# A hybrid RWKV and attention layer: GpSimd's tiles behind the key norm, final states ahead of the third pair's operands, and the MLP norm by a ones matrix

## Chip, core and metric

The kernel runs on one core of one Trainium2 chip. The metric is the device time of one execution in microseconds. TensorE is called PE, VectorE DVE, ScalarE ACT, GpSimd POOL and SyncE SP.

## What is computed

One layer for 512 prompt tokens and 8 sequences of 8 decode tokens. RWKV-7 mixing and differential attention run side by side on the same normalised input; gates merge them; a squared-ReLU MLP and a final norm follow. Of the reference, what the change touches:

```python
kk = hs((k * lp['k_k']).astype(f32))
kk = kk / jnp.maximum(jnp.linalg.norm(kk, axis=-1, keepdims=True), 1e-12)
...
def step(S, inp):                     # one token of the RWKV scan
    sa = jnp.einsum('bhij,bhj->bhi', S, a_t)
    S = S * w_t[:, :, None, :] + sa[..., None] * b_t[:, :, None, :] + v_t[..., None] * k_t[:, :, None, :]
    return S, jnp.einsum('bhij,bhj->bhi', S, r_t)
...
x = x + m @ lp['w_out']
hn = rmsnorm(x, lp['g_ffn'], NORM_EPS)
x = x + jnp.square(jax.nn.relu(hn @ lp['w_up'])) @ lp['w_down']
return x, S, ...                      # S: the final states, an output
```

The norm's factor commutes with the squared ReLU: with m the mean square plus epsilon, the MLP's sum is 1/m times that of the unscaled row. So the kernel multiplies x by m (M2), adds the products of the unscaled row, and multiplies by 1/m (R2) at the end.

## The kernel before

Tokens lie on the free axis: 576 columns, in two spans of 288 (HALF). Weights come in pieces through a ring of three loads, and each is split into a high and a low part (ACT makes `hi`, L179, DVE `lo`, L180), so that every product is three matmuls. Small helpers record the instructions, and the trace shows their lines: `act` L58, `tt` L61, `stt` L66, `ts` L69, `mm` L72, `tr` (transpose on PE) L76. `bank` hands out one of three PSUM banks.

The RWKV part works on four pairs of heads, hp 0 to 3 (first to fourth pair). `rwkv(hp)` is a generator in six stages, cut by `yield`:

1. The key norm: squares `sq`, their sums by PE into `pn`, `nr` by DVE, the power -1/2 by GpSimd (L760), the copy `nb` over 64 columns a head by GpSimd (L763), and PE transposes of it into `pk` and `pks`. PE makes the adapters' products `pw` and `pa` meanwhile. DVE scales the keys (`sq` again), builds `rkp`, whose block sums are `pbn`, and the operands KB and ST. GpSimd zeroes half of ST (L818). PE multiplies them into `pA`.
2. The values SVU; KBt; the start states `s0` of the decode rows, loaded over SP (L859) into one of two buffers; their products `pI`. GpSimd fills two parts of SVU (L871, L872).
3. The inverse of the triangular blocks, TT; GpSimd zeroes parts of it (L923, L924).
4. The final states of the decode rows: GpSimd makes `vm` (L933), PE `pF`, DVE adds and scales in the buffer of `s0`, and a DMA from GpSimd's queue writes it out (L941).
5. and 6. The mean and variance of the output rows, and the output.

`chain(pr)` (L991) runs the recurrence over eight prompt chunks and the decode chunk for two pairs at once; the chunk steps are short dependent products with DVE and ACT copies between them (`pch`, `R`, `SVU`, `S`). The code below the generators (L1081 on) calls stages and chains, with `take(n)` to put n matmuls of waiting dense products (`ps_z`, `ps_g`) between. Each product has a priority, and a scheduler orders every engine's instructions by priority and by the order in which they are written; `tc.issue_after` ties instructions to one given.

Ahead of the MLP, `acc` holds the squares of x summed over the eight blocks of 128 channels. `up_pair` makes seven products of twelve matmuls each (`ua`, `ub`, `uc`, `ud`, `ux`; a 2x2 product scheme), `down` the products `ps_dn`. After the first `up_pair`, `colsum` sums `acc` over the partitions with ten narrow matmuls into `pst`, DVE makes m (128x5) and its reciprocal r, and `spread` turns each back into rows of 576 by five PE transposes (`pb_M`, `pb_R`) and five ACT copies.

Of the kernel before, what the change touches and what calls it, by code (L numbers as in the profile page):

```python
# [8 lines left out]
F32 = mybir.dt.float32  # L9
# [6 lines left out]
P = 128  # L16
D = 1024
# [11 lines left out]
HALF = ((0, 288), (288, 288))  # L29
# [7 lines left out]
C_ID, C_OB, C_M, C_MS, C_LM, C_I32, C_HS, C_SEL, C_MB, C_CM, C_END = (  # L37
    0, 128, 256, 384, 512, 672, 704, 706, 738, 746, 748)
# [3 lines left out]
def tile_hybrid_step(ctx, tc, xT, xsT, ktab, vtab, s0T, ptab, w_in, vecs, w2a2, g2, lamv,  # L42
# [3 lines left out]
    PE, VE, AE, GE = nc.tensor, nc.vector, nc.scalar, nc.gpsimd  # L46
    PS = bass.MemoryType.PSUM

    def pool(name, bufs=1, stack=ctx, **kw):
        return stack.enter_context(tc.tile_pool(name=name, bufs=bufs, **kw))  # L50
# [4 lines left out]
    ring = {"job": 0}  # L55

    def act(out, in_, func=AF.Copy, **kw):
        ring["act"] = AE.activation(out=out, in_=in_, func=func, **kw)  # L58

    def tt(out, a, b, op, eng=None):  # L60
        ins = (eng or VE).tensor_tensor(out=out, in0=a, in1=b, op=op)  # L61
        if eng is None:
            ring["tt"] = ins

    def stt(out, a, s, b, op0, op1):
        VE.scalar_tensor_tensor(out=out, in0=a, scalar=s, in1=b, op0=op0, op1=op1)  # L66

    def ts(out, a, s1, op0, s2=None, op1=ALU.bypass, eng=None):
        (eng or VE).tensor_scalar(out=out, in0=a, scalar1=s1, scalar2=s2, op0=op0, op1=op1)  # L69

    def mm(out, lhsT, rhs, start=True, stop=True):
        ring["mm"] = PE.matmul(out=out, lhsT=lhsT, rhs=rhs, start=start, stop=stop)  # L72
        return ring["mm"]

    def tr(out, in_, idn):
        ring["mm"] = PE.transpose(out=out, in_=in_, identity=idn)  # L76

    def bc(ap, shape):
        return ap.broadcast_to(shape)
# [3 lines left out]
    FEED, LATE, FILL = -1000000, 500000, 1000000  # L83

    @contextmanager
    def prio(at):
        was, tc.cur_priority = tc.cur_priority, at
        yield
        tc.cur_priority = was

    MUL, ADD, SUB, MAX = ALU.mult, ALU.add, ALU.subtract, ALU.max
# [7 lines left out]
    stat = pool("stat", 2)  # L99

    def bank(name):
        return psw.tile([P, 512], F32, tag="w", name=name)

    def tbank(name):
        return psc.tile([P, 512], F32, tag="t", name=name)
# [6 lines left out]
    c = const.tile([P, C_END], F32, name="cst_sb")  # L112
# [3 lines left out]
    ones1 = const.tile([P, 1], F32, name="ones1")  # L116
# [8 lines left out]
    onesP = const.tile([P, P], F32, name="onesP")  # L125
# [90 lines left out]
    def take(n):  # L216

        while waiting and n:
            if next(waiting[0], None) is None:
                waiting.pop(0)  # L220
            else:
                n -= 1
# [11 lines left out]
    def colsum(out, src, sel, n):  # L234

        for t in range(5):
            m = min(P, NT - t * P)
            mm(out[:m, t * n:(t + 1) * n], src[:, t * P:t * P + m], sel)
# [6 lines left out]
    def spread(dst, r, name):  # L245

        for t in range(5):
            m = min(P, NT - t * P)
            pb = bank(f"pb_{name}_{t}")
            tr(pb[:, :m], bc(r[:m, t:t + 1], [m, P]), ident[:m, :m])  # L250
            act(dst[:, t * P:t * P + m], pb[:, :m])
# [19 lines left out]
    with tc.tile_pool(name="xin", bufs=2, reuse_waits="tile") as xin:  # L271
        xt = [xin.tile([P, NT], F32, name=f"x{k}", bufs=1) for k in range(KT)]
        xs_ = xin.tile([P, KT, NB], F32, name="xs", bufs=1)
        acc = xin.tile([P, NT], F32, name="acc", bufs=1)
# [3 lines left out]
        for k in range(0, KT, 4):  # L278
            for j in range(3):
                with prio(FEED + 1000 + 10 * k + j):  # L280
                    name = f"raw_{'qkv'[j]}0_{k}"
# [26 lines left out]
        pst = tbank("pst1")  # L308
# [356 lines left out]
    for h in range(HB):  # L665
        if h:
            qkv(h)
        for cc in range(2):
            GE.tensor_copy(
                out=qbd[64 * cc:64 * cc + 64, :, h, 8 * cc:8 * cc + 8],  # L670
                in_=qT[64 * cc:64 * cc + 64, h, NPR:].rearrange("p (b q) -> p b q", b=NB))
# [47 lines left out]
    def ch(a):  # L719
        return a.rearrange("p (c t) -> p c t", t=64)  # L720
# [21 lines left out]
    def rwkv(hp):  # L742
        e = hp % 2
        own = pair.setdefault(hp // 2, {})
        hs = slice(hp * P, (hp + 1) * P)
        r, k, vv = Pt[hp], Pt[4 + hp], Pt[8 + hp]
# [8 lines left out]
        for t, o in enumerate(toks):  # L755
# [4 lines left out]
        GE.tensor_tensor(out=nr, in0=nr, in1=mhalf[:, :10], op=ALU.pow)  # L760

        nb = rt.tile([P, 5, P], F32, tag="G", name=f"nb{hp}", bufs=3)
        GE.tensor_copy(out=nb.rearrange("p t (a d) -> p (t a) d", a=2),  # L763
                       in_=nr.rearrange("p (a o) -> p a o", o=1).broadcast_to([P, 10, 64]))
        u = tmp("u")
        aa = tmp("aa")
# [47 lines left out]
        for par, rows in halves:  # L814
            stt(KB[rows, :, par], ch(aa)[rows], 0.5, ch(pinv)[rows], MUL, MUL)
            tt(KB[rows, :, 1 - par], ch(k2)[rows], ch(pinv)[rows], MUL)
            st = rb_.tile([P, NCH, 2, 64], F32, tag=f"ST{par}", name=f"ST{par}_{hp}")
            GE.memset(st[64 - 64 * par:128 - 64 * par], 0.0)  # L818
            stt(st[rows, :, 0], ch(kk)[rows], -1.0, ch(pm)[rows], MUL, MUL)
            tt(st[rows, :, 1], ch(r)[rows], ch(pe)[rows], MUL)  # L820
            ST.append(st)
# [4 lines left out]
        for par in range(2):  # L826
            rows = slice(64 * par, 64 * par + 64)
# [14 lines left out]
        SVU = own["SVU"][:, :, e]  # L842
# [23 lines left out]
        for par in range(2):  # L866
            rows = slice(64 * par, 64 * par + 64)
            for a in range(2):
                act(ST[par][rows, 8, a].rearrange("p (b t) -> p b t", b=NB),
                    pI[rows, 0:P].rearrange("p (b a t) -> p b a t", b=NB, a=2)[:, :, a])  # L870
            GE.tensor_copy(out=SVU[rows, 8, par], in_=c[rows, C_ID + 64 * par:C_ID + 64 * par + 64])  # L871
            GE.memset(SVU[rows, 0, par], 0.0)  # L872

        yield

# [21 lines left out]
        for l in range(1, 5):  # L897

            n = NCH if l < 3 else 8
# [6 lines left out]
        TT = rb_.tile([P, NCH, 64], F32, tag="TT", name=f"TT{hp}")  # L906
# [12 lines left out]
        for b0, b1 in quads:  # L919
            act(TT[b0, :8, 32:64], pC[b0, :256].rearrange("p (c s) -> p c s", c=8))  # L920
            act(TT[b0, :, 0:32], Y[b0])
            act(TT[b1, :, 32:64], Y[b1])
            GE.memset(TT[b0, 8:, 32:64], 0.0)  # L923
            GE.memset(TT[b1, :, 0:32], 0.0)  # L924

        own[e] = ST, KBt, TT, ABR, pc
        yield
# [140 lines left out]


    gens = [rwkv(hp) for hp in range(4)]  # L1070

    def run(*stages):
        for hp in stages:
            while Pt[8 + hp] is None:
                take(2)
            next(gens[hp], None)
# [7 lines left out]
    take(106)  # L1084
    run(1)
    chain(0)
    run(2, 0, 1)
    take(190)
    run(2, 3)
    take(85)  # L1090
# [49 lines left out]
    R2 = fp.tile([P, NT], F32, name="R2")  # L1140
    M2 = fp.tile([P, NT], F32, name="M2")
    acc = fp.tile([P, NT], F32, name="acc2")
# [146 lines left out]
    def down(c, ds):  # L1289

        q, half = divmod(c, 2)
        his, los = ([qs[4 * c + k][:, i] for k in range(4)] for i in range(2))
        for d in ds:
            if c == 0:
                with prio(FEED + 1000 * ring["job"] + 150):
                    tt(ya[:, d], ya[:, d], M2, MUL)

            def ev(ps, t0, n, d=d):
                o = ya[:, d, t0:t0 + n]
                tt(o, o, ps, ADD)  # L1300
            dense(w_down[q, d][:, 4 * half:4 * half + 4], 4, his, los, HALF, ev, f"dn{c}{d}")

    for ch in range(8):
        for i in range(2):
            up_pair(4 * ch + 2 * i)
            if ch == 0 and i == 0:
                with prio(FILL + 1000 * ring["job"] + 999):

                    pst = bank("pst2")
                    colsum(pst, acc, ones1, 1)  # L1310
                with prio(FEED + 1000 * ring["job"]):
                    m2 = stat.tile([P, 5], F32, tag="r", name="m2")
                    r2 = stat.tile([P, 5], F32, tag="s", name="r2")
                    VE.memset(m2, 1.0)
                    ts(m2[:, 0:4], pst[:, 0:4], 1.0 / D, MUL, 1e-6, ADD)
                    ts(m2[:64, 4:5], pst[:64, 4:5], 1.0 / D, MUL, 1e-6, ADD)
                    VE.reciprocal(out=r2, in_=m2)
                with prio(FILL + 1000 * ring["job"] + 1999):
                    spread(M2, m2, "M2")
                with prio(FILL + 1000 * ring["job"] + 9999):  # L1320
                    spread(R2, r2, "R2")
            if 0 < ch < 7:
                down(ch - 1, range(4 * i, 4 * i + 4))

# [2 lines left out]
    rows = []  # L1327
    for d, n in enumerate((None, "t1", "b11", "t2", "b21", "t3", "b22", "t4")):
        if n:
            t = fp.tile([P, 2, 4, 288], F32R, tag=f"h_{n}", name=f"w3_{d}", bufs=1)  # L1330
            t = t.rearrange("p i k t -> p (i k t)")
# [6 lines left out]
    for t0, n in LAST:  # L1338
# [41 lines left out]
        for i, src in enumerate([acc[:, span]] + last):  # L1380
            pst = bank(f"pst3{t0}{i}")
# [20 lines left out]
        for d in range(KT):  # L1402
# [4 lines left out]
            if d + 1 in ends:  # L1407
                i = ends.index(d + 1)
# [119 lines left out]
```

## Time and profile before

| | us |
|---|---|
| median of three runs | 998.73 (998.32 to 999.4) |
| profiled execution | 1002.8 |
| its span, first to last instruction | 1001.0 |
| PE busy | 968.1 |
| DVE busy | 691.0 |
| ACT busy | 496.0 |
| GpSimd busy | 88.6 |

The mean granted TensorE clock is 0.988 of full speed. In a row of the timeline stand the start, the duration, the engine, the line, the operation, output and input by the program's names, the tile's shape and the count; a bracket holds the idle time of the engine ahead of it and what ended that. In the chain of waits stand start, duration and what the time went to. The windows give busy time by engine in a stretch.

### The profile page before, as it was taken

To read this page: it belongs to the slowest core of one execution; us is meant where nothing else is said; L and a number is where in the kernel's file an instruction comes from. 1 tells how busy PE (TensorE), PEld (TensorE's weight loads), DVE (VectorE), ACT (ScalarE), POOL (GpSimd) and SP (SyncE) were. 2 spreads that over 40 slices of the span, in tenths; PEclk is the share of its full clock that TensorE was granted. 3 is DMA by queue.
4 is the path that set the end of the run, shared out by engine and by line. 5 is a ranking of instruction groups with operands and counts; after the bars stand their busy time and mean duration, and the time that the engine had idled before them with its cause. 6 is when DMAs were issued, how large, how long until landed. Compare 5 with 4: busy or idle time off the path is not lost.

```text
span 1001.0 us, 24421 instructions
## 1 busy us (share of the span) xinstructions
PE 968.1 (97%) x10012; PEld 916.7 (92%) x10012; DVE 691.0 (69%) x1459; ACT 496.0 (50%) x1094; POOL 88.6 (9%) x171
## 2 busy tenths in 40 slices
PE   8999999899999989999999999999999999999996
PEld 8999998898887878888889999999999999999996
DVE  6698566774946759536589798966666666666744
ACT  6576455354445344444334666644444444444732
POOL 2511001401002231001110000000000000000001
PEclk9999999999999989999999999999999999999998
DMA  7322673211121225222377642222222222221402
GB/s 264 135 74 76 211 219 112 70 56 54 44 66 38 69 87 160 76 64 102 120 225 237 216 132 86 84 95 86 85 94 86 85 85 85 85 84 44 135 3 95
DMA packets 50833, 105.75 MB, mean 106 GB/s; under 512 B 6066, under 2 KB 8114, under 8 KB 50594
## 3 DMA queue, kind: packets, MB, share of 16 engines
q1 hardware_dynamic: 47442, 96.95, 30.2%
q0 software_dynamic: 1648, 5.35, 1.5%
q10 hardware_dynamic: 1632, 1.89, 0.5%
q8 instruction: 79, 1.29, 0.5%
q14 instruction: 32, 0.26, 0.1%
HBM read 89.38 MB, written 14.78 MB: 104 GB/s over the span
## 4 chain that ended last, share of the span: by engine, by line
PE 88%; DVE 4%; ACT 4%; issue 1%; DMA 1%; POOL 1%; SPq 0%; DVEq 0%; ACTq 0%; POOLq 0%
PE ps_dn L72 21%; PE ps_g L72 10%; PE ps_z L72 8%; PE ua L1247 5%; PE ux L1247 5%; PE ps_wo L72 4%; PE pch L1007 3%; PE ps_brb L72 3%; PE ps_k L72 3%; PE uc L1247 3%; PE ud L1247 3%; PE ub L1247 3%; PE ps_bra L72 3%; PE ps_q L72 2%; PE ps_v L72 2%; PE pA L72 2%
## 5 line engine op out<-in xcount | busy, mean ns | idle before, releaser
L72 PE MATMUL ps_dn<-q,hi_dn 128*128 128x288 f32 x768 | 154.7, 296 | 0.0
L72 PEld LDWEIGHTS ps_dn<-q,hi_dn 128*128 128x128 f32 x768 | 122.7, 188 | 1.4
L72 PE MATMUL ps_dn<-q,lo_dn 128*128 128x288 f32 x384 | 113.1, 295 | 0.0
L72 PE MATMUL ps_g<-xl,hi_g 128*128 128x288 f32 x256 | 79.8, 312 | 0.0
L72 PE MATMUL ps_g<-xh,hi_g 128*128 128x288 f32 x256 | 79.5, 311 | 0.0
L72 PE MATMUL ps_g<-xh,lo_g 128*128 128x288 f32 x256 | 78.3, 306 | 0.0
L72 PEld LDWEIGHTS ps_dn<-q,lo_dn 128*128 128x128 f32 x384 | 72.0, 188 | 0.0
L72 PE MATMUL ps_z<-xh,lo_z 128*128 128x288 f32 (+1 forms) x224 | 69.2, 310 | 0.0
L72 PE MATMUL ps_z<-xh,hi_z 128*128 128x288 f32 (+1 forms) x224 | 68.0, 304 | 0.0
L72 PE MATMUL ps_z<-xl,hi_z 128*128 128x288 f32 (+1 forms) x224 | 67.1, 300 | 0.0
L61 DVE TENSOR_TENSOR ya<-ya,ps_dn 128x288 f32<-128x288 f32 x96 | 43.3, 451 | 29.4 <-PE ps_dn L72 29.4
L58 ACT ACTIVATE hi_dn<-raw_dn 128x512 fp32r<-128x512 f32 x48 | 30.1, 627 | 57.0 <-PE ps_dn L72 57.0
L1247 PE MATMUL ua<-h_b,hi 128*128 128x288 f32 x256 | 53.2, 298 | 0.0
L1247 PE MATMUL ux<-h_t,hi 128*128 128x288 f32 x256 | 52.3, 296 | 0.0
L58 ACT ACTIVATE c<-c 128x288 f32<-128x288 f32 x112 | 48.3, 439 | 7.5 <-DVE c L61 5.9
L72 PEld LDWEIGHTS ps_g<-xh,hi_g 128*128 128x128 f32 x256 | 48.8, 191 | 3.1 <-issue 1.6
L72 PEld LDWEIGHTS ps_g<-xl,hi_g 128*128 128x128 f32 x256 | 49.1, 192 | 1.5
L72 PEld LDWEIGHTS ps_g<-xh,lo_g 128*128 128x128 f32 x256 | 49.0, 191 | 1.0
L58 ACT ACTIVATE hi<-a 128x1024 fp32r<-128x1024 f32 (+1 forms) x32 | 27.1, 845 | 42.0 <-PE ps_dn L72 34.3
L72 PE MATMUL ps_dn<-q,w 128*128 128x320 f32 (+1 forms) x336 | 46.3, 297 | 0.0
L61 DVE TENSOR_TENSOR lo<-s,hi 128x1024 fp32r<-128x1024 f32 x32 | 39.2, 1224 | 10.2 <-ACT hi L58 10.0
L72 PEld LDWEIGHTS ps_dn<-q,w 128*128 128x128 f32 x336 | 45.3, 190 | 0.1
(393 smaller groups left out, 2788.8 us busy)
## 6 DMA issues: line engine op xcount, KB each, us to landing
a<-in_w_up_dram SPq DMA_DIRECT2D x32, 512.0 KB, 3.3
raw_dn<-in_w_down_dram SPq DMA_DIRECT2D x64, 256.0 KB, 2.8
raw_g<-in_w_in_dram SPq DMA_DIRECT2D x32, 256.0 KB, 3.0
raw_z<-in_w_in_dram SPq DMA_DIRECT2D x28, 256.0 KB, 3.0
gt_d<-gg SPq DMA_DIRECT2D x16, 288.0 KB, 2.3
g<-gt_d SPq DMA_DIRECT2D x16, 288.0 KB, 3.6
kp<-in_ktab_dram SPq DMA_DIRECT2D x16, 256.0 KB, 3.7
vp<-in_vtab_dram SPq DMA_DIRECT2D x16, 256.0 KB, 3.9
```

Source lines behind the costliest of these rows:

```text
L58: ring["act"] = AE.activation(out=out, in_=in_, func=func, **kw)
L61: ins = (eng or VE).tensor_tensor(out=out, in0=a, in1=b, op=op)
L72: ring["mm"] = PE.matmul(out=out, lhsT=lhsT, rhs=rhs, start=start, stop=stop)
L1007: ring["mm"] = PE.matmul(out=ps[rows, e], lhsT=lhs, rhs=rhs, start=first and e == 1, stop=True, skip_group_check=True)
L1247: ring["mm"] = PE.matmul(out=ps[:, :288], lhsT=l[:, k], rhs=hb[blk][:, h, k], start=start and i == 0, stop=i == 11, skip_group_check=skip)
```

## The change

Three edits. GpSimd's fills of ST (first pair), and of SVU and TT (first two pairs), are tied behind the copy `nb` of the same pair. Stage 4 of the first two pairs is written ahead of stage 1 of the third. And the MLP norm's column sums are made by a 128x128 matrix of ones, which leaves the sum on every partition at once: M2 comes from it by one operation of DVE on each span, and R2 by a full-width reciprocal, two chunks of the MLP later.

```diff
-        GE.tensor_copy(out=nb.rearrange("p t (a d) -> p (t a) d", a=2),
+        own["nb"] = GE.tensor_copy(out=nb.rearrange("p t (a d) -> p (t a) d", a=2),
...
-            GE.memset(st[64 - 64 * par:128 - 64 * par], 0.0)
+            with tc.issue_after(own["nb"].ins) if hp == 0 else nullcontext():
+                GE.memset(st[64 - 64 * par:128 - 64 * par], 0.0)
...
-            GE.tensor_copy(out=SVU[rows, 8, par], in_=c[rows, C_ID + 64 * par:C_ID + 64 * par + 64])
-            GE.memset(SVU[rows, 0, par], 0.0)
+            with tc.issue_after(own["nb"].ins) if hp < 2 else nullcontext():
+                GE.tensor_copy(out=SVU[rows, 8, par], in_=c[rows, C_ID + 64 * par:C_ID + 64 * par + 64])
+                GE.memset(SVU[rows, 0, par], 0.0)
...
-            GE.memset(TT[b0, 8:, 32:64], 0.0)
-            GE.memset(TT[b1, :, 0:32], 0.0)
+            with tc.issue_after(own["nb"].ins) if hp < 2 else nullcontext():
+                GE.memset(TT[b0, 8:, 32:64], 0.0)
+                GE.memset(TT[b1, :, 0:32], 0.0)
...
     chain(0)
-    run(2, 0, 1)
+    run(0, 1, 2)
...
             if ch == 0 and i == 0:
-                with prio(FILL + 1000 * ring["job"] + 999):
-
-                    pst = bank("pst2")
-                    colsum(pst, acc, ones1, 1)
-                with prio(FEED + 1000 * ring["job"]):
-                    m2 = stat.tile([P, 5], F32, tag="r", name="m2")
-                    r2 = stat.tile([P, 5], F32, tag="s", name="r2")
-                    VE.memset(m2, 1.0)
-                    ts(m2[:, 0:4], pst[:, 0:4], 1.0 / D, MUL, 1e-6, ADD)
-                    ts(m2[:64, 4:5], pst[:64, 4:5], 1.0 / D, MUL, 1e-6, ADD)
-                    VE.reciprocal(out=r2, in_=m2)
-                with prio(FILL + 1000 * ring["job"] + 1999):
-                    spread(M2, m2, "M2")
-                with prio(FILL + 1000 * ring["job"] + 9999):
-                    spread(R2, r2, "R2")
+                for t0, n in HALF:
+                    with prio(FILL + 1000 * ring["job"] + 999):
+                        pm2 = bank(f"pm2{t0}")
+                        mm(pm2[:, :n], onesP, acc[:, t0:t0 + n])
+                    with prio(FEED + 1000 * ring["job"]):
+                        ts(M2[:, t0:t0 + n], pm2[:, :n], 1.0 / D, MUL, 1e-6, ADD)
+            if ch == 2 and i == 0:
+                for t0, n in HALF:
+                    with prio(FEED + 1000 * ring["job"] + 900):
+                        VE.reciprocal(out=R2[:, t0:t0 + n], in_=M2[:, t0:t0 + n])
```

GpSimd's order in the first pair, before (`ob_d` is the attention's output, numbers count the program's tiles):

```order
L711 DMA ob_d<-obs 128x4x64
L818 MEMSET ST_0_2814 64x1152
L818 MEMSET ST_0_2820 64x1152
L760 TENSOR_TENSOR nr_2749<-nr_2749,mhalf 128x10
L871 COPY SVU_2861<-cst_sb 64x64
L872 MEMSET SVU_2861 64x64
L763 COPY nb_2752<-nr_2749 128x640
```

and after:

```order
L711 DMA ob_d<-obs 128x4x64
L760 TENSOR_TENSOR nr_2749<-nr_2749,mhalf 128x10
L763 COPY nb_2752<-nr_2749 128x640
L819 MEMSET ST_0_2814 64x1152
L819 MEMSET ST_0_2820 64x1152
L873 COPY SVU_2861<-cst_sb 64x64
L874 MEMSET SVU_2861 64x64
```

The power and the copy of the first pair now stand directly behind the output's DMA, and the fills follow.

GpSimd's order in the chain of the first two pairs, before; `nr` and `nb` are the third pair's, `vm` belongs to the first (two) and second pair, and the last `vm`, the fills of SVU and the writes of the two states come only behind the chain's own output:

```order
L760 TENSOR_TENSOR nr_4872<-nr_4872,mhalf 128x10
L763 COPY nb_4875<-nr_4872 128x640
L61 TENSOR_TENSOR vm_4984<-SVU_2861,cst_sb 128x512
L61 TENSOR_TENSOR vm_4986<-SVU_2861,cst_sb 128x512
L61 TENSOR_TENSOR vm_4994<-SVU_2861,cst_sb 128x512
L818 MEMSET ST_2_4942 64x1152
```

and after:

```order
L61 TENSOR_TENSOR vm_4857<-SVU_2861,cst_sb 128x512
L61 TENSOR_TENSOR vm_4859<-SVU_2861,cst_sb 128x512
L61 TENSOR_TENSOR vm_4867<-SVU_2861,cst_sb 128x512
L61 TENSOR_TENSOR vm_4869<-SVU_2861,cst_sb 128x512
L944 DMA out_Ss_dram<-s_0_2891 128x512
L760 TENSOR_TENSOR nr_4892<-nr_4892,mhalf 128x10
L763 COPY nb_4895<-nr_4892 128x640
L944 DMA out_Ss_dram<-s_1_3905 128x512
```

All four `vm` and the first write now stand ahead of the third pair's power and copy, and the second write right behind them.

PE's order at the same place, after; before, the four `pF` stood behind the third pair's `pA`, outside the chain (`pch` with ABR leaves a chunk, with TT solves it):

```order
L1010 MATMUL pch_4646<-SVU_2861,ST_0_2814 64x64
L72 MATMUL pF_4856<-vm_4859,KBt_2875 64x512
L72 MATMUL pF_4866<-vm_4867,KBt_3889 64x512
L1010 MATMUL pch_4646<-R_4655,TT_4520 64x64 x2
L1010 MATMUL pch_4646<-R_4655,TT_3678 64x64 x2
L1010 MATMUL pch_4596<-SVU_2861,ABR_3839 64x64 x2
L1010 MATMUL pch_4596<-SVU_2861,ABR_2824 64x64 x2
L1010 MATMUL pch_4607<-SVU_2861,ABR_3839 64x64 x2
L1010 MATMUL pch_4607<-SVU_2861,ABR_2824 64x64 x2
L72 MATMUL pF_4866<-vm_4869,KBt_3889 64x512
L72 MATMUL pn_4878<-cst_sb,sq_4876 128x2 x5
```

The final states' products stand between the steps of the chain, and the third pair's norm sums `pn` behind the last of them.

## The prediction

> **What bounds the kernel now.** I read the page's busy times and the cores view first, then the waits of TensorE (PE) by releaser, then the timeline around the longest of them.
>
> ```profile
> PE 968.1 (97%) x10012; PEld 916.7 (92%) x10012; DVE 691.0 (69%) x1459; ACT 496.0 (50%) x1094; POOL 88.6 (9%) x171
> core 0: 1001.0 us, clock 0.988
> ```
>
> PE is busy in 968.1 of 1001.0 us, GpSimd (POOL) in 88.6. So nothing is won by less GpSimd work as such; what can be won is an idle stretch of PE, the half-speed stretch behind one, or PE work that goes. The change touches three places, one of each kind. The profiled execution took 1002.8 us, 1.8 beyond its span and 4.1 above the median of the runs, 998.73. I work out differences in the profile and take them off the median.
>
> **Place 1: the first pair's `nr` and `nb` go ahead of the two ST memsets.** The timeline of before, start and duration first; a bracket is the idle time before, with its releaser:
>
> ```profile
> 175.88 0.16 DVE L69 TENSOR_SCALAR nr<-pn 128x10 f32<-128x10 f32 x1
> 176.25 0.80 POOL L711 DMA_DIRECT2D ob_d<-obs  x1 [1.34 <-DVE nr L69]
> 177.09 2.17 POOL L818 MEMSET ST<- 64x1152 f32 x2
> 179.23 2.19 POOL L760 TENSOR_TENSOR nr<-nr,mhalf 128x10 f32<-128x10 f32 x1
> 180.88 0.43 DVE L61 TENSOR_TENSOR Z<-ps_z,R 128x288 f32<-128x288 f32 x1
> 181.66 0.71 POOL L763 COPY nb<-nr 128x640 f32<-128x640 f32 x1
> 182.42 1.12 PE L76 MATMUL pk<-cst_sb,nb 128*128 128x128 f32 x4 [2.67 <-POOL nb L763]
> 183.57 0.75 DVE L66 SCALAR_TENSOR_TENSOR sq<-P,vec,pk 128x512 f32<-128x512 f32 x1 [2.26 <-PE pk L76]
> ...
> 246.82 1.25 POOL L763 COPY nb<-nr 128x640 f32<-128x640 f32 x1
> ...
> 311.24 0.60 PE L76 MATMUL pk<-cst_sb,nb 128*128 128x128 f32 x4
> ```
>
> `nr` was there at 176.04, but GpSimd did 2.17 us of memsets first, so `nb` landed at 182.37. Without them: the DMA issue ends at 177.05, the power takes 2.19, the copy 0.71, and `nb` lands at 179.95 (at 180.5 if the copy takes the 1.25 us that the second pair's took). PE, idle from 179.75, waits 0.2 to 0.75 instead of 2.67, and its four `pk` may take 0.60 again instead of 1.12: PE gains up to 2.47 + 0.52 = 3.0. VectorE (DVE) waited 2.26 for `pk`. It could start `sq` at 181.31, when `Z` ends, and by then `pk` is done (180.5 + 0.6 = 181.1 even in the slow case), so its wait goes whole. What counts afterwards the windows show (length, then busy us of PE, PEld, DVE, ACT, POOL, then the clock):
>
> ```profile
> core 0: us, PE busy (x) PEld busy (x) DVE busy (x) ACT busy (x) POOL busy (x), PEclk, DMA share, GB/s
> 180.00:186.00 6.00, 3.58 (x18) 3.59 (x19) 3.73 (x8) 1.69 (x3) 5.66 (x12) 0.72 0.00 0
> 186.00:200.00 14.00, 14.00 (x102) 13.35 (x101) 13.19 (x22) 4.11 (x7) 1.02 (x5) 1.00 0.26 76
> ...
> 380.00:400.00 20.00, 17.83 (x200) 16.37 (x198) 19.59 (x33) 9.68 (x20) 0.00 (x0) 1.00 0.56 174
> ```
>
> From 186 to 200 PE is busy in all 14.00 us and DVE in 13.19, so both are dense and the smaller gain stays: DVE's 2.26. If DVE only lengthened its 0.81 of idle there, 1.45 would be left. Bounds -1.45 and -3.0; I take **-2.3**. The memsets of ST, of SVU and of TT come later by the 2.9 us of power and copy; GpSimd is nearly free after 186 (1.02 of 14), so they hide there.
>
> **Place 2: the final states of the first two pairs move into the chain of the first two, ahead of the third pair's operands.** The chain of waits (start, duration), and the rows of the same groups where nothing held them:
>
> ```profile
> 358.64 3.58 DMA out_Ss_dram<-s
> 362.37 3.44 DMA s<-in_s0T_dram
> 365.95 1.82 PE pI L72 x32
> 367.77 2.22 PE pn L72 x10
> 369.99 2.13 PE ps_g L72 x8
> ...
> 305.56 1.21 PE pn L72 x10
> ...
> 419.73 1.04 PE pI L72 x32
> ```
>
> The third pair's start states reuse a buffer whose old content must first be written out. So the write (3.58) and the read (3.44) stand in series before `pI`. Now the timeline and its window:
>
> ```profile
> 365.95 1.82 PE L72 MATMUL pI<-ST,s 64*64 64x16 f32 x32 [2.41 <-DMA s<-in_s0T_dram]
> ...
> 365.00:372.00 7.00, 6.05 (x51) 6.04 (x52) 0.86 (x2) 1.80 (x6) 1.65 (x1) 0.58 0.03 10
> ...
> 387.83 1.24 PE L72 MATMUL pbn<-rkp,cst_sb 128*128 128x288 f32 x4 [1.50 <-DVE rkp L66]
> ```
>
> PE was idle 2.41 us, and the granted clock is 0.58 over the window behind it. With the write moved into the chain both loads are done long before. PE then gains 2.41, 1.82 - 1.04 = 0.78 in `pI` and 2.22 - 1.21 = 1.01 in `pn`: 4.20. Eight `ps_g` behind them, 2.13 against 1.07 at the 0.134 us each that twelve take below (1.60 for `uc`), would make it 5.26; but this last gain comes behind `pn`, whose sums open the fourth pair's work on DVE, and DVE is busy in 19.59 of the 20 us from 380 to 400. PE already waits 1.50 for DVE at `pbn`. So 4.20 counts, and the 1.06 is waited for again.
>
> [...]
>
> What place 2 costs, in the chain of the first two pairs:
>
> ```profile
> 309.80 2.50 POOL L61 TENSOR_TENSOR vm<-SVU,cst_sb 128x512 f32<-128x512 f32 x2
> ...
> 358.64 1.16 POOL L941 DMA_DIRECT2D out_Ss_dram<-s  x2 [3.20 <-DVE s L61]
> ...
> 370.35 1.99 POOL L760 TENSOR_TENSOR nr<-nr,mhalf 128x10 f32<-128x10 f32 x1 [10.55 <-DVE nr L69]
> ```
>
> GpSimd's order there becomes four `vm` of 1.25, one output issue of 0.58, the power of 1.99, the copy `nb` of about 0.7. Before, power and `nb` stood first. `pF`, which needs a `vm`, now stands in the middle of the chain; PE has only two pairs of `ps_g` and a few small chain products between the decode chunk's solve and the first `pF`. I let these hide the SVU copies and let PE wait one `vm`, 1.2. Each later `vm` lies beside a `pF` or a chain step. `pk` comes some 2.7 us of power and copy after `pn`, and has `ps_g`, four small products of the adapters and a chain step in front: a wait of 0.3. Sum 1.5, bounds 0 and the whole 4.2. The 2.7 us is the one row far from zero in it, and I lean to the low end because PE's list fills most of it. DVE takes eight operations on `s` along. On SyncE's queue the two state loads now wait for the output of the states with a gate's output and the next weight loads behind them; those loads refill a slot three pieces ahead of their use, so I cost the delay at nothing, and if that cover is gone it lies within the bound of 4.2. Net **-2.7** (0 to -4.2).
>
> **Place 3: the MLP norm by a ones matrix.** PE has no gap there; its work shrinks. Timeline and windows:
>
> ```profile
> 176.57 0.65 PE L72 MATMUL pw<-P,wl 128*128 128x288 f32 x2
> 177.54 0.65 PE L72 MATMUL pw<-P,wl 128*128 128x288 f32 x2
> ...
> 601.30 1.60 PE uc L1247 x12
> ...
> 612.66 0.28 PE L72 MATMUL pst<-ones,acc 128*128 128x1 f32 x2
> 615.53 0.27 PE L76 MATMUL pb_M<-cst_sb,m 128*128 128x128 f32 x1
> 617.95 0.43 PE L1247 MATMUL ub<-h_t,hi 128*128 128x288 f32 x2
> ...
> 620.00:630.00 10.00, 10.00 (x74) 9.66 (x74) 9.29 (x15) 5.12 (x12) 0.00 (x0) 1.00 0.25 79
> ```
>
> From the first `pst` to the first `pb_M` 2.87 us go by, 1.60 of them the twelve `uc`: the column sums cost 1.27. From there to `ub` 2.42 with twelve `ua`: the spread of M costs 0.82, and that of R, the same five transposes a little later, as much again. Out: 2.91. In: two fp32 products of 128x288, like a `pw` and a `pa`, of which one of each stands between the two rows above, 0.97. That is -1.94. DVE is busy 9.29 of 10 here, so it may give less: bounds 0 and -1.94; I take **-1.9**, since PE is never idle in that window.
>
> The full-width reciprocal, two of 128x288, is new. The groups view (busy us, mean ns) and DVE's idle time at its new place:
>
> ```profile
> L558 DVE RECIPROCAL rz<-z 128x2 f32<-128x2 f32 x16 | 2.6, 160 | 4.2 <-ACT sc L58 4.0
> L1317 DVE RECIPROCAL r<-m 128x5 f32<-128x5 f32 x1 | 0.2, 176 | 0.0
> ...
> 651.82 0.45 DVE L61 TENSOR_TENSOR ya<-ya,ps_dn 128x288 f32<-128x288 f32 x1 [1.15 <-PE ps_dn L72]
> 656.02 0.46 DVE L61 TENSOR_TENSOR u<-ub,p 128x288 f32<-128x288 f32 x1 [2.98 <-PE ub L1247]
> ```
>
> Three more columns cost 16 ns more, so 288 cost 0.16 + 286 x 0.0053 = 1.7 us at most by that slope, 0.45 at least like the addition of that width. I take 1.7, the only rows of that operation. Two are 3.4, against 1.15 + 2.98 of idle time where they stand: nothing, and up to 1.1 if each delays an addition by 1.7 - 1.15. [...]
>
> **The rivals.**
> A, slower: GpSimd falls behind in the chain. Copies of `nb` took 0.71 and 1.25 us, so beside a busy DVE its work can nearly double. With `vm` at 2.5 and power and copy to match, PE waits over the 2.41 us that lowered the clock, at the first `pF` and again at `pk`. Each costs about 2.5 of wait and 0.78 + 1.01 + 1.06 of half speed, 5.3; two are 10.6, more than the 2.3 + 4.2 + 1.9 = 8.4 won: 1000.9. It decides from a wait of 2.4 on at both places. Against it: `vm` at 309.80 ran beside DVE at 1.25. 0.05.
> B, the gap moves to the fourth pair's `pbn`: PE comes 5.26 earlier, DVE's `rkp` 4.20, and the wait grows from 1.50 to 2.56, past 2.41. The clock falls there; 1.8 as at `pI` and `pn` are paid again: 993.6. 0.17.
> [...] 0.13.
> D, all PE time comes back (-3.0, -5.26 + 1.5, -1.9): 990.1; it needs DVE to find slack in the dense windows. 0.10.
> E, it doesn't do what it says: the time before `pI` and `nb` is waited for at the next DVE-bound operand, and place 3 at DVE: 998.0 or so. For it: 13.19 of 14 and 19.59 of 20. Against: DVE's own waits are part of the gap. 0.05.
>
> **How the numbers follow.** The forecast has 0.50: 998.73 - 2.3 - 2.7 - 1.9 = 991.8 (995.9 in a profile like this one). The range reaches down to 989.0, which holds D and the forecast's own low end, and up to 995.5, which holds B, C and place 2 at one half; it leaves out A, E and some of the tails. Faster by over 0.2% (2.0 us, about what a measurement of this kernel tells from no change) is forecast, B, C, D: 0.90; same is E, 0.05; slower is A, 0.05.
>
> **What would show it.** Place 1: `pk` of the first pair starting near 180.3 with an idle time under 0.8, and `sq` without its 2.26. Place 2: no wait at `pI`, clock 1.00 around it, an idle time of 1 to 1.5 at a `pF` in the chain, under 0.5 at `pk`. Place 3: the first MLP pair of products shorter by 1.9, reciprocals of 1.7 with no PE idle time behind them. It is wrong if the clock falls at a new place (below 0.9 in the windows of the chain or of the fourth pair's `pbn`), or if the dense windows of DVE start no earlier.

## The result, and the profile after

The changed kernel takes 993.14 us, median of five runs (990.76 to 993.64), beside 998.32 (997.01 to 999.4, five runs) of the kernel before on the same chip: a ratio of 0.994, 95% interval 0.9919 to 0.9961, so 6.0 us less with an interval of 3.9 to 8.1. Two later measurements gave 0.9939 (0.9923 to 0.9956) and 0.9927 (0.9908 to 0.9947). The forecast was 991.8.

The profiled executions alone would say more: the spans differ by 9.4 us, 1001.0 and 991.6. The one of before was among its slowest; of the 29 runs of before beside the first experiments below one took as long. Part of what its profile shows did not come back in other executions of the same instructions, and which part is the main finding of the experiments.

Busy times and the core's line after:

```profile
PE 964.5 (97%) x9996; PEld 913.4 (92%) x9996; DVE 694.3 (70%) x1459; ACT 495.1 (50%) x1084; POOL 91.0 (9%) x171
core 0: 991.6 us, clock 0.989
```

PE is busy 3.6 us less. The span shrank by 9.4, so most of it was idle time of PE.

Place 1 in the timeline after:

```profile
176.33 0.80 POOL L711 DMA_DIRECT2D ob_d<-obs  x1 [1.34 <-DVE nr L69]
177.15 2.20 POOL L760 TENSOR_TENSOR nr<-nr,mhalf 128x10 f32<-128x10 f32 x1
179.34 1.36 DVE L777 TENSOR_TENSOR_SCAN cum<-reset,u 128x576 f32<-128x576 f32 x1
179.41 1.80 POOL L763 COPY nb<-nr 128x640 f32<-128x640 f32 x1
181.27 0.66 PE L76 MATMUL pk<-cst_sb,nb 128*128 128x128 f32 x4 [1.44 <-POOL nb L763]
181.96 0.75 DVE L66 SCALAR_TENSOR_TENSOR sq<-P,vec,pk 128x512 f32<-128x512 f32 x1 [0.91 <-PE pk L76]
```

The order is the one announced: the power right behind the output's DMA, the copy right behind the power. But the copy, now beside DVE's scan, took 1.80 us and not 0.71. So PE still waited 1.44 where 0.2 to 0.75 was forecast, and DVE 0.91 where nothing was.

Place 2 after, from the chain on:

```profile
304.71 4.43 POOL L61 TENSOR_TENSOR vm<-SVU,cst_sb 128x512 f32<-128x512 f32 x4 [41.58 <-DVE SVU L1025]
306.19 0.64 PE L72 MATMUL pF<-vm,KBt 128*64 128x512 f32 x1 [0.35 <-POOL vm L61]
315.81 0.33 PE L76 MATMUL pk<-cst_sb,nb 128*128 128x128 f32 x1 [0.60 <-POOL nb L763]
320.11 0.45 PE L1010 MATMUL pch<-SVU,KBt 128*64 128x64 f32 x8 [0.24 <-ACT SVU L58]
360.10 1.11 PE L72 MATMUL pI<-ST,s 64*64 64x16 f32 x32
361.14 1.28 PE L72 MATMUL pn<-cst_sb,sq 128*128 128x2 f32 x10
380.04 1.24 PE L72 MATMUL pbn<-rkp,cst_sb 128*128 128x288 f32 x4 [1.11 <-DVE rkp L66]
```

`pI` no longer waits; it takes 1.11 us instead of 1.82, and `pn` starts 1.04 behind it. The new waits in the chain are 0.35 for the first `vm`, 0.60 for `nb` and 0.24 for an SVU copy, 1.19 together. But the chain of before had waits of its own for SVU copies, which are gone, since the `pF` stand there now:

```profile
313.88 0.45 PE L1007 MATMUL pch<-SVU,KBt 128*64 128x64 f32 x8 [0.28 <-ACT SVU L58]
317.51 0.69 PE L1007 MATMUL pch<-SVU,ST 128*64 128x64 f32 x16 [1.11 <-ACT SVU L58]
```

That is 1.39, so by its waits the chain got no longer. The wait at `pbn` went from 1.50 to 1.11. DVE's `nr` of the fourth pair, 2.4 us early by place 1, is 7.6 us early there: 362.45 against 370.03.

But the windows around `pn` (as before: length, busy times, then the clock before the last two numbers) show that half speed did not vanish with the idle time:

```profile
360.00:362.00 2.00, 2.00 (x42) 1.87 (x40) 0.28 (x1) 0.80 (x4) 0.00 (x0) 1.00 0.03 8
362.00:364.00 2.00, 2.00 (x12) 2.00 (x12) 0.81 (x2) 1.26 (x4) 1.23 (x1) 0.67 0.02 4
364.00:366.00 2.00, 2.00 (x6) 1.43 (x6) 1.63 (x5) 1.46 (x3) 1.48 (x3) 0.50 0.36 127
```

PE is busy in all 2.00 us of each, and the clock falls to half behind the narrow products of `pI` and `pn`. The stretch is shorter, though. Over the same 16 us, before and after:

```profile
362.00:378.00 16.00, 13.59 (x157) 12.39 (x157) 6.88 (x16) 6.67 (x17) 6.81 (x8) 0.79 0.17 54
362.00:378.00 16.00, 16.00 (x104) 14.90 (x104) 12.54 (x25) 9.82 (x19) 7.09 (x8) 0.89 0.19 64
```

A mean of 0.79 over 16 us is some 6.7 us at half clock, one of 0.89 some 3.5.

Place 3 after: the ones products, DVE's operations and the reciprocals.

```profile
605.03 1.14 PE L72 MATMUL pm<-acc,onesP 128*128 128x288 f32 x4
606.27 0.81 DVE L69 TENSOR_SCALAR M<-pm 128x288 f32<-128x288 f32 x2
640.50 1.94 DVE L1319 RECIPROCAL R<-M 128x288 f32<-128x288 f32 x1
646.43 0.46 DVE L61 TENSOR_TENSOR u<-ub,p 128x288 f32<-128x288 f32 x1 [1.22 <-PE ub L1250]
...
630.00:650.00 20.00, 20.00 (x152) 20.00 (x152) 18.23 (x29) 7.86 (x15) 0.00 (x0) 1.00 0.25 79
```

A reciprocal takes 1.94 us (the second, at 643.27, takes 1.95), PE is busy in 20.00 of 20 us around them, and DVE still waits 1.22 afterwards. They are hidden.

### The profile page after: what moved, and what is told of

The parts are those of the page before. It is cut to its first block, busy times and chain, and to the rows that moved or that the text cites. A ratio compares the mean times of both kernels' runs of the same rounds, so it can differ in the third digit from the quotient of the medians.

```text
span 991.6 us, 24377 instructions
## 1 busy us (share of the span) xinstructions
PE 964.5 (97%) x9996; PEld 913.4 (92%) x9996; DVE 694.3 (70%) x1459; ACT 495.1 (50%) x1084; POOL 91.0 (9%) x171
## 4 chain that ended last, share of the span: by engine, by line
PE 83%; DVE 6%; issue 6%; ACT 3%; POOL 1%; DMA 0%; SPq 0%; DVEq 0%; POOLq 0%; ACTq 0%
PE ps_dn L72 21%; PE ps_z L72 8%; PE ps_g L72 7%; PE ux L1250 5%; PE ua L1250 5%; PE ps_wo L72 4%; PE ps_brb L72 3%; PE ps_k L72 3%; PE ub L1250 3%; PE ud L1250 3%; PE ps_bra L72 3%; PE uc L1250 3%; PE pch L1010 2%; PE ps_q L72 2%; PE ps_v L72 2%
```

## The experiments

The theory at the start was the prediction's: three independent gains. The rivals: each is waited for again (E, B), the reciprocals cost something (C), and, new, the clock's falls are not tied to the instructions, so that two profiles don't compare. Each kernel ran beside the kernel before on the same chip; ratios are to that. An edit is shown against the kernel after unless it says otherwise.

**The first part alone.** GpSimd's fills behind `nb`, the rest as before.

```diff
     chain(0)
-    run(0, 1, 2)
+    run(2, 0, 1)
...and the MLP norm by colsum and spread
```

> Only GpSimd's fills behind nb (place 1). Theory: DVE's wait for pk falls from 2.26 to 0.9 and the half-speed stretch at 182 to 186 goes, so 2.3 us come off: about 996.0 where before is 998.3, and nothing changes from 350 us on. Rival (the saved time is waited for again at the next operand that DVE makes): within 0.5 us of before. Rival (the clock falls somewhere else instead, as it does at 243 to 247 us in the whole change, where before had no fall): 0.6 us given back, about 996.6, with a granted clock below 0.9 in a window between 240 and 250 us.

Measured 999.0 us (12 runs) beside 998.89 (29 runs): 1.0, interval 0.9986 to 1.0014. Yet its profile is 2.4 us ahead of that of before at 187 us, keeps 2.0 or more of it up to 350 us, and shows no fall of the clock between 240 and 250. Neither the theory nor a gain eaten later explains this; the profile it is compared with may be the odd one. The next two kernels, which have place 1 as before, show that it is.

**The second and the third part alone.** These two edits are shown against the kernel before.

```diff
     chain(0)
-    run(2, 0, 1)
+    run(0, 1, 2)
```

> Only the final states of the first two pairs ahead of the third pair's operands (place 2). Theory of the prediction: 4.2 off at pI and pn, 1.5 back in the chain, so 2.7 off: about 995.6. Reading of the whole change's profile, whose lag against before grows from 2.1 to 7.0 us over this place: 4.9 off, 993.4. Rival (part of what the profile of before shows there is a half-speed stretch that most executions do not have): 1.5 to 2.5 off, 996 to 997. In every case no wait of PE for the state load is left, and waits at a pF of about 0.35 and at pk of about 0.6.

995.47 us (12 runs): 0.9968, interval 0.9957 to 0.9979, 3.2 us less. Nothing waits for the state load.

```diff
-                    colsum(pst, acc, ones1, 1)
...
+                        mm(pm2[:, :n], onesP, acc[:, t0:t0 + n])
...the norm part of the change alone
```

> Only the MLP norm by the ones matrix (place 3). Theory: ten narrow products and ten transposes go, two fp32 products of 128x288 come, 1.9 off: 996.4. Rival (the reciprocals, 1.94 us each in the profile of the whole change, hold up DVE's additions and give part of it back): 0.8 off or less, over 997.5. The lag against before must stay at zero up to 605 us and change only in the first MLP products and around the reciprocals.

997.65 us (12 runs): 0.9987, interval 0.9971 to 1.0003; 1.3 us less, within the noise by itself.

Both hold place 1 as the kernel before has it. Its rows in the states' kernel, the norm's kernel and, third, the whole change without part 1 (below), with the window behind each:

```profile
182.14 0.66 PE L76 MATMUL pk<-cst_sb,nb 128*128 128x128 f32 x4 [2.66 <-POOL nb L763]
182.00:186.00 4.00, 3.86 (x30) 3.86 (x31) 3.16 (x8) 1.82 (x3) 3.62 (x11) 1.00 0.00 0
```

```profile
182.35 0.66 PE L76 MATMUL pk<-cst_sb,nb 128*128 128x128 f32 x4 [2.66 <-POOL nb L763]
182.00:186.00 4.00, 3.65 (x28) 3.65 (x29) 2.95 (x7) 1.79 (x4) 3.65 (x9) 1.00 0.00 0
```

```profile
181.52 0.65 PE L76 MATMUL pk<-cst_sb,nb 128*128 128x128 f32 x4 [2.66 <-POOL nb L763]
182.00:186.00 4.00, 4.00 (x32) 4.00 (x31) 3.67 (x9) 2.44 (x4) 3.56 (x10) 1.00 0.00 0
```

The same wait of 2.66 as before's 2.67, and the clock stays at 1.00 in all three; in the profile of before it is 0.60 in that window:

```profile
182.00:186.00 4.00, 3.58 (x18) 3.59 (x19) 2.42 (x6) 0.68 (x2) 3.66 (x9) 0.60 0.00 0
```

DVE's wait for `pk` was 1.79 in these three, not 2.26; 0.91 of it is left with place 1, 0.9 less. A second, smaller part was not foreseen: DVE's `u` (128x576), just ahead of the scan, takes 0.80 in these three and 0.46 in nine profiles with place 1; what slows it is not shown. What both give is seen at DVE's first `rkp`, an operand behind `sq`, in the norm's kernel and in the first kernel:

```profile
192.43 0.81 DVE L66 SCALAR_TENSOR_TENSOR rkp<-P,vec,k 128x576 f32<-128x576 f32 x1
191.08 0.81 DVE L66 SCALAR_TENSOR_TENSOR rkp<-P,vec,k 128x576 f32<-128x576 f32 x1
```

`nr` started at 175.81 and 175.86, so the way from there is 16.62 and 15.22 us: place 1 is worth 1.4 with full clock. In the profile of before that way is 17.64; the fall costs another 1.0. 1.4 lies at the edge of the interval of the first kernel.

The states' kernel shows the other side of it. Its `pbn`, and the windows behind:

```profile
380.88 1.38 PE L72 MATMUL pbn<-rkp,cst_sb 128*128 128x288 f32 x4 [1.82 <-DVE rkp L66]
382.00:386.00 4.00, 4.00 (x84) 3.63 (x83) 3.42 (x6) 1.80 (x4) 0.00 (x0) 0.59 0.76 244
386.00:390.00 4.00, 4.00 (x71) 3.80 (x72) 3.84 (x8) 2.27 (x5) 0.00 (x0) 1.00 0.90 281
```

Here the clock fell behind a wait of 1.82, as rival B had it; six other profiles with place 2 have a wait of 1.81 or 1.82 at the same place and kept it at 1.00. In the remaining four (1.10 to 1.18) the clock had fallen some 17 us earlier, at `pI` and `pn`, and PE came to `pbn` later.

The two kernels with place 2 as before (the first and the norm's) kept a wait at `pI`, of 2.26 and 3.06, and the clock fell behind it in both, for some 6.7 and 10.2 us (means of 0.79 and 0.68 between 362 and 378 us). So with the wait it fell in three profiles of three; in the eleven without the wait it fell there in four, for 3.4 us each. The runs spread less without it too: the two kernels ran from 995.1 to 1001.4 and from 994.6 to 1001.5, the states' kernel from 994.1 to 997.2, twelve runs each.

**The whole change again, twice,** without an edit.

> The whole change once more, beside its three parts on the same chip. If the parts are independent, its gain is the sum of theirs: theory 2.3 + 2.7 + 1.9 = 6.9; measured so far 5.2. If the clock's falls move with the phase, the profile of this execution shows them at other places than the first profile (243, 277 and 363 us), or not at all; if they are tied to the instructions, at the same ones.

992.26 us (6 runs), 0.9939. The profile has the falls of the first, at 243, 277 and 363 us.

> The whole change a third time, as the yardstick for the other two of this call: ratio to before 0.994, as measured twice, within its interval; each execution with some of the clock's falls at 8, 243, 277 and 363 us, none of them in all executions.

991.83 us (6 runs), 0.9927. In this profile the clock is 1.00 in the windows from 240 to 248, 274 to 282 and 358 to 368. The same program had three falls in one execution and none of them in another; the fall at 8 us, in front of all of this, is in both.

**Leaving one part out.** First without part 1, which is the second and the third part together:

```diff
-            with tc.issue_after(own["nb"].ins) if hp == 0 else nullcontext():
-                GE.memset(st[64 - 64 * par:128 - 64 * par], 0.0)
+            GE.memset(st[64 - 64 * par:128 - 64 * par], 0.0)
...SVU and TT likewise
```

> The whole change without place 1 (GpSimd's fills where before has them). In its profile place 1 gains 2.0 to 2.5 us, but alone it measured 0.0 (plus or minus 1.4). Theory: place 1 is worth about 1.2, what its idle time gives where the half-speed stretch at 182 to 186 does not follow, as in the profiles of the two kernels that kept it; so this kernel is 1.2 above the whole change, about 993.6 beside 992.4. Theory of the prediction: 2.3 above, 994.7. Rival (place 1 is worth nothing): equal to the whole change.

993.82 us (6 runs): 0.9942, interval 0.9925 to 0.9958. Against the whole change's 0.9939 and 0.9927, measured at other times, that is 0.3 to 1.5 us: near the theory's 1.2, not apart from nothing. On its own chip the nearest kernel to the whole change is the one with the reciprocals moved (below): 991.8 (989.78 to 992.62) against 993.82 (993.37 to 995.25), so 2.0 for place 1 there, if the move costs nothing.

Then without part 3:

> The whole change without place 3 (the MLP norm as before). Theory: 1.9 us above the whole change of the same call. Rival (the full-width reciprocals or DVE's added work give it back): within 0.5 us of it. The lag against the whole change must open between 605 and 650 us and stay after.

The edit puts back `colsum` and `spread`. 993.69 us (991.9 to 994.76) beside the whole change's 991.83 (991.15 to 993.04) on the same chip: 1.9, the theory's number. The lag opens where it should. The first and the last of the four weight sums of one form that DVE makes between 590 and 660 us, in the whole change (its third measurement) and then without part 3:

```profile
601.14 0.68 DVE L61 TENSOR_TENSOR s<-a 128x512 f32<-128x512 f32 x1
...
653.61 0.69 DVE L61 TENSOR_TENSOR s<-a 128x512 f32<-128x512 f32 x1
```

```profile
600.74 0.68 DVE L61 TENSOR_TENSOR s<-a 128x512 f32<-128x512 f32 x1
...
655.18 0.68 DVE L61 TENSOR_TENSOR s<-a 128x512 f32<-128x512 f32 x1
```

Over this stretch the one takes 52.47 us and the other 54.44: 1.97 of difference, with reciprocals and all. The first pair of profiles gives 52.47 after and 54.42 before, the norm's kernel 52.46 and the first kernel 54.44.

**The reciprocals where DVE is full.** In the first chunk instead of the third:

```diff
-            if ch == 2 and i == 0:
+            if ch == 0 and i == 1:
                 for t0, n in HALF:
```

> The whole change with the two reciprocals of 1.94 us in the MLP's first chunk, where DVE is busy 9.97 of 10 us, instead of the third, where it has idle time. Theory (at the third chunk they are hidden): here they hold up the additions, PE waits, 1 to 3 us above the whole change. Rival (they cost as much where they are now, or DVE has room in both places): equal to the whole change, within 0.5 us.

991.8 us (6 runs): 0.9914, interval 0.9897 to 0.9932. The theory fell. The first of the two in their new place:

```profile
606.92 1.95 DVE L1319 RECIPROCAL R<-M 128x288 f32<-128x288 f32 x1
```

Moving 3.9 us of DVE work into a stretch where DVE was busy 9.97 of 10 cost nothing: DVE's other work there (weight splits for later products) was ahead of its use and slid back (the first `lo_dn` by 10 us, from 609.10 in the whole change's second profile to 619.46) and caught up by 645 us. PE's products stand within 0.3 us of that profile's both before and behind the stretch. The reciprocals are free in both places.

**The first pair's state alone ahead.**

```diff
     chain(0)
-    run(0, 1, 2)
+    run(0, 2, 1)
```

> The whole change, but with only the first pair's final state ahead of the third pair's operands, the second pair's behind them as before. Theory (the state load alone made the wait at pI, and only the first pair's buffer matters for it): no wait at pI is left, two vm less stand ahead of nb, the wait at pk of 0.60 goes; equal to the whole change or up to 0.7 better. Rival (part of place 2's gain is that both pairs' pF, vm and DVE work fill the chain and leave the stretch at 350 us): 0.5 to 2 us above the whole change.

990.64 us (6 runs): 0.9917, interval 0.9897 to 0.9937. No wait at `pI` is left, so the first pair's buffer was the one that mattered. The wait at `pk` did not go; it is 0.91:

```profile
309.80 0.62 POOL L944 DMA_DIRECT2D out_Ss_dram<-s  x1 [4.84 <-DVE nr L69]
310.44 1.99 POOL L760 TENSOR_TENSOR nr<-nr,mhalf 128x10 f32<-128x10 f32 x1
313.42 0.66 PE L76 MATMUL pk<-cst_sb,nb 128*128 128x128 f32 x4 [0.91 <-POOL nb L763]
```

Not the second pair's `vm` but the write's issue, the power and the copy behind `nr` hold `pk` up; and `nr` itself comes at 309.42, 1.7 us behind the end of `pn`, since DVE has other work first (in the whole change it comes at once).

**The attention output's DMA on SyncE's queue.**

```diff
-    nc.gpsimd.dma_start(out=ob_d.rearrange("h p t -> p h t")[:, :, NPR:], in_=obs)
+    nc.sync.dma_start(out=ob_d.rearrange("h p t -> p h t")[:, :, NPR:], in_=obs)
```

> The whole change with the attention output's DMA on SyncE's queue, so that GpSimd takes the power right when nr is there (176.1 in place of 177.15). Theory: nb lands 1.0 us earlier, PE's wait of 1.44 at pk falls to 0.5 and DVE's of 0.91 to nothing: 0.5 to 0.9 us below the whole change. Rival (DVE's work behind is what ends that stretch, or the copy nb is slowed by the DVE scan beside it whenever it comes, 1.80 us against 0.71): no difference.

990.99 us (6 runs): 0.9915, interval 0.9897 to 0.9933. Its timeline at place 1:

```profile
175.16 1.96 POOL L760 TENSOR_TENSOR nr<-nr,mhalf 128x10 f32<-128x10 f32 x1 [1.20 <-DVE nr L69]
177.18 0.72 POOL L763 COPY nb<-nr 128x640 f32<-128x640 f32 x1
178.63 0.60 PE L76 MATMUL pk<-cst_sb,nb 128*128 128x128 f32 x4
179.93 0.74 DVE L66 SCALAR_TENSOR_TENSOR sq<-P,vec,pk 128x512 f32<-128x512 f32 x1
...
190.08 1.24 PE L72 MATMUL pbn<-rkp,cst_sb 128*128 128x288 f32 x4 [0.77 <-DVE rkp L66]
```

Both waits are gone. The copy, now ahead of the scan, takes 0.72 again. `sq` is 2.0 us earlier than in the whole change, of which 1.0 came before this place by chance (the clock at 8 us). And part of PE's gain is waited for again at the next operand of DVE, as the rival had it: `pbn` of this pair waits 0.77, where the whole change has no wait.

**Both of the last together.**

> The whole change with only the first pair's final state ahead, and the attention output's DMA on SyncE's queue. Theory (both gains are of different places and add): 1 to 1.5 us from the one and about 1 from the other, 2 to 2.5 below the whole change of the same call. Rival (each measured low by the clock's chance falls): within 0.7 us of it.

The edit is the two shown. 990.89 us (990.06 to 992.46) beside 991.83 (991.15 to 993.04) of the whole change, on the same chip; 0.9916 (0.9896 to 0.9936) against 0.9927. That is 0.9 us, less than the 2 to 2.5 of the theory and nearer to the rival: part of what each seemed to gain alone may be which executions were met. It is no faster than each edit alone (0.9915 and 0.9917 beside 0.9916), and its lead over the whole change isn't certain.

**The clock behind narrow products.** Runs of narrow products (128x2) between dense products of the MLP, whose sums are not used; the rest is the whole change:

```diff
+            if i == 0 and 1 <= ch < 7:
+                with prio(FILL + 1000 * ring["job"] + 9500):
+                    pz = bank(f"pz{ch}")
+                    for _ in range((0, 10, 15, 20, 30, 40, 60)[ch]):
+                        mm(pz[:, 0:2], onesP, c[:, C_HS:C_HS + 2])
```

> The whole change with runs of 9, 14, 19, 29, 39 and 59 narrow fp32 products (128x2, about 0.115 us each) put between dense products of the MLP, one run in each of chunks 1 to 6; their sums are not used. In no execution so far did the clock fall in the dense MLP. In the whole change it fell at 363 and at 243 us with PE idle for less than 0.2 us, behind some 2.3 us of narrow products (pI and pn, or pWc, pn and pC). Theory (the gate counts what the array does, not whether PE waits): the granted clock falls behind the longer runs, from 29 (3.3 us) or 39 (4.5 us) on, with PE busy all through, and perhaps behind 19 (2.2 us). Rival (it counts idle time alone, and the two falls had another cause): clock 1.00 throughout the MLP.

1052.69 us, one run, for the added work. The first run of nine and the second of fourteen (two passes each, so the count is double; the first product of each ten or fifteen runs by itself, some 1.8 us ahead), with the windows behind:

```profile
649.08 2.07 PE L72 MATMUL pz<-cst_sb,onesP 128*128 128x2 f32 x18
652.00:656.00 4.00, 4.00 (x32) 4.00 (x31) 2.62 (x5) 3.19 (x7) 0.00 (x0) 1.00 0.06 23
...
699.31 3.18 PE L72 MATMUL pz<-cst_sb,onesP 128*128 128x2 f32 x28
700.00:703.00 3.00, 3.00 (x28) 3.00 (x28) 0.61 (x2) 0.89 (x2) 0.00 (x0) 1.00 0.50 175
703.00:707.00 4.00, 4.00 (x21) 4.00 (x21) 2.05 (x3) 1.72 (x3) 0.00 (x0) 0.58 0.01 4
```

Behind 2.07 us nothing happens; behind 3.18, and behind all four longer runs, the clock falls, with PE busy 3.00 of 3 and 4.00 of 4 us. A product takes 0.23 us, not the 0.115 of the expectation, so the fall comes at fourteen instead of twenty-nine, at the length that was expected. The rival, that idle time alone counts, is out. This is one execution; that 2.07 us is too short is seen once.

The falls in the profiles of before, of after, of the whole change's third measurement, of the kernel without part 3, of the two edits together and of the narrow products have one more thing in common. But for the last one, which the end of the execution cuts, each lasts 3.41 us or a multiple, and in one execution they start whole multiples of 3.41 us apart: at 7.69, 181.76, 277.34 and 366.08 us in the profile of before, which is 51, 28 and 26 such steps. A guess from this is that each step counts as a whole, so that how a wait lies across the steps matters; no run shows it by itself. At place 1 in the profile of before, the step in front of the fall and the fall:

```profile
178.35:181.76 3.41, 1.40 (x10) 1.10 (x8) 2.52 (x3) 1.63 (x4) 3.41 (x5) 1.00 0.00 0
181.76:185.17 3.41, 2.75 (x12) 2.76 (x13) 1.60 (x5) 0.49 (x1) 3.07 (x9) 0.50 0.00 0
```

PE was busy 1.40 of 3.41 there. In the three kernels that kept the clock the same wait lay otherwise, and the emptiest step has 1.73, 1.85 and 1.96. That fits, but does not settle it: at `pbn` the states' kernel fell behind a step with 1.59, and the whole change's third profile did not behind one with 1.60.

## Why the prediction came out as it did

The sign, the mechanisms of the three places and two of three sizes were right; the forecast was 6.9 us, the measurement 5.2 in the medians and 6.0 by the ratio of the runs, and the two later ratios make it 6.1 and 7.3.

- **Place 1, -2.3: the term that was mis-sized.** Alone 0.0 (plus or minus 1.4), left out of the whole 0.3 to 1.5 across chips and 2.0 on one, by the rows 1.4 with full clock. Two steps failed. "PE ... waits 0.2 to 0.75": the copy took 1.80 beside DVE's scan, longer than the 1.25 taken as the slow case, and PE waited 1.44. And "DVE waited 2.26 for `pk`" was read from an execution in which the clock had fallen; with the same wait of 2.66 and full clock it is 1.79. In the first two profiles themselves the gain is 2.4, near the forecast, and 1.0 of it is that fall. The bounds of -1.45 and -3.0 were drawn for an execution with the fall; 1.4, without it, lies just outside them.
- **Place 2, -2.7: right in sum, and in part by luck.** Alone -3.2 (1.1 either way). The new waits in the chain, 0.35 + 0.60 + 0.24 = 1.2, are near the 1.5 forecast, but the wait for `vm` was a third of what was taken, that for `nb` twice, and that for SVU not named. And the prediction looked only at what the chain would get: the 0.28 + 1.11 that it lost are as much, so the net cost was about nothing. Of the gain, the 2.41 of idle time is certain (2.26 and 3.06 in two other kernels that still wait). That leaves about 0.6 (1.1 either way) for half speed and all the rest, where 1.8 was taken: the fall comes each time with the wait, but it did not go each time without it. In two of three profiles of the whole change the clock fell at 363 us without any wait. A cost taken too high and a gain taken too high cancelled.
- **Place 3, -1.9: right.** 1.97 by the rows, 1.9 in the medians (1.3, with zero inside its interval, alone). The reciprocals were forecast at 1.7 each and took 1.94; they are hidden, as said, and, beyond what was said, they would be hidden in the full stretch too.
- **The rivals.** A: `vm` took 1.1 each and no wait came near 2.4. B: the wait at `pbn` grew, but from 1.50 to 1.82 and not to 2.56 (seven profiles); in the four in which the clock had already fallen at `pI` and `pn` it was 1.10 to 1.18. The clock did fall there in one of the seven, behind 1.82. So the point set for it, a wait over 2.41, was wrong in both directions: 2.66 was passed over three times at place 1, 1.82 was not. C, that the reciprocals hold up the additions, has 0.13 and a place in the range; no run shows such a cost: without part 3 the kernel takes 1.9 us more, and with the reciprocals moved into the full stretch it takes 991.8. E is out by the states' kernel, whose interval leaves out 1.0. D did not come: at place 1 PE still waited 1.44.
- **The clock.** The prediction took the 1.8 of half speed at `pI` and `pn` to come back together with the idle time of 2.41. The runs show that idle time is not all of it: the clock fell to half behind 3.18 us of narrow products with PE busy all through, the falls of six profiles start on steps of 3.41 us, and whether a fall comes behind a wait differs from execution to execution: behind 2.26, 2.41, 2.67 and 3.06 it came, behind 2.66 three times not. What was wrong was to count on the stretch coming back whole.

What stays open: why the first kernel shows nothing at all, where rows say 1.4, the edge of its interval; why the clock falls behind one wait and not behind another of the same length; and whether the last version (990.89) truly beats the change (991.83).

## What to carry to other kernels

Before pricing a half-speed stretch from one profile, look at a second execution of the same kernel: a fall of the clock behind a short wait can be a chance of that execution (here one profile of four at place 1, but three of three at `pI`). Price the wait itself as certain and the stretch by how often it is met. And when work moves into a place, count the waits that it fills there as well as those that it brings. When work of one engine is moved, look which operation of another runs beside it at the new place: a GpSimd copy of 0.71 us became 1.80 beside a DVE scan, and moving it two us earlier gave that back, though DVE's next operand then took 0.77 of it.

## What the runs showed of the hardware

- The TensorE clock fell to half with TensorE busy all the time, behind 3.18 us of 128x2 products, but not behind 2.07. In six profiles a fall lasted 3.41 us or a multiple, but for the one that the end cuts, and the falls of one execution started whole multiples of 3.41 us apart.
- Waits of 2.66 us left the clock at 1.00 in three executions and a wait of 2.67 was followed by 0.60 in a fourth, the instructions being the same.
- The GpSimd copy of 128x640 took 0.71 us behind DVE's scan of 128x576, 0.72 ahead of it and, in six profiles, 1.80 beside it. DVE's `u` of 128x576 at the same place took 0.80 or 0.81 in the four profiles with the old order of GpSimd and 0.46 in nine with the new one.
- DVE's reciprocal of 128x288 took 1.94 us beside 0.18 for 128x5: 6.2 ns for each further column; from 128x2 to 128x5 the slope had been 5.3.
